# The function table of the RMS norms: one named set with logarithm and exponential, asked for ahead of the logarithm

## The chip, the cores and the metric

One Trainium2 chip, of which the kernel uses one core. The metric is the device time of one launch in microseconds, the median of several executions. Engines as the profile names them: PE is the matrix engine (TensorE) and PEld its weight loads, DVE is VectorE, ACT is ScalarE, POOL is GpSimd, SP is SyncE, which issues most DMAs. Each engine works through its own list of instructions in order and waits for the others by semaphores.

## The reference

One inference step of a two-layer decoder trunk for a prompt of 512 positions and a sample group of 8 x 4 positions, D_MODEL 1024, all in 32-bit floating point. What matters here are the norms: four per layer and group.

```python
def rms_norm(x, g):
    x32 = x.astype(jnp.float32)
    return x32 * lax.rsqrt(jnp.mean(x32 * x32, axis=-1, keepdims=True) + NORM_EPS) * g

def decoder_layer(x, start, st, prm):
    h = rms_norm(x, prm['g_mix_pre'])
    p_rw, p_s5, p_gdn, p_swa = split_cols(h @ prm['w_in'], PROJ_SPLITS)
    ...                                   # four mixers: RWKV-7, S5, gated DeltaNet, window attention
    mix = jnp.concatenate([o_rw, o_s5, o_gdn, o_swa], axis=-1) @ prm['w_out']
    x = x + rms_norm(mix, prm['g_mix_post'])
    h = rms_norm(x, prm['g_mlp_pre'])
    f = jnp.square(jax.nn.relu(h @ prm['w_up'])) @ prm['w_down']
    x = x + rms_norm(f, prm['g_mlp_post'])
    return x, ...
```

## The kernel before

Activations lie transposed: 128 partitions by 8 blocks of features by columns of positions. The 544 columns are cut into two halves, of 256 prompt columns and of 256 prompt plus 32 sample columns (288). Each dense product (`dense`, L1697) streams its weights from HBM in parts of 128 x 512: SP issues the load of `wraw` (L1656), ACT casts it to `whi` (L231), DVE forms the rest `wlo` (L235), and PE takes three groups of four matmuls for each part, whi and wlo with the two parts of the activation (L219; tiles `h` and `f` by name). The buffers are few (5 wraw, 3 whi, 3 wlo), so ACT, DVE and PE run in step. The four mixers add many small matmuls, elementwise work and DMAs. While one half is in a mixer, the other half's dense products fill PE.

A scheduler that has its own timeline sets the order on every engine: instructions are listed with priorities (`PRIO`, `ahead`, `section`), and the scheduler places each on its engine when its model has it ready. `after` (L185) adds an order between two instructions for the scheduler alone, with no semaphore at run time. A change of one instruction's place can so move others.

A norm is done in four steps. The squares of the features are summed into `sums` by ACT (Square, tile `d`) and POOL (L235). PE multiplies `sums` with a column of 1/1024 (`mean`), which leaves the mean in PSUM on all partitions. `rsqrt` (L1565) makes of it the factor `sums` = exp(-0.5 ln(mean + eps)) with two ACT instructions, `sums<-ps,eps` and `sums<-sums`. DVE then scales the row (L244, `d` or `c`), and what follows (a residual sum, or the cast to `h` or `f` by ACT, L231) goes on from there. There are 16 such norms; they are called norm 1 to norm 16 here, in the order in which ACT comes to them. Norm 1 is the first half's first norm, which has its own code in `first` (L1581), norm 2 the second half's; norms 3 to 15 are those between the products, and norm 16 is the last one, ahead of the output.

ACT evaluates a function from a set of tables that has to be loaded, by an ACT_TABLE_LOAD. Where the kernel doesn't ask for a set, the build puts a load in front of an activation whose function the set loaded last doesn't hold, after the order is fixed. Logarithm and exponential are so taken from two sets. Besides the norms the mixers use Exp, Tanh, Ln and Sin; copies, casts, squares and Relu need no load of their own.

Of the kernel before, what the change touches and what calls it, by code (L numbers as in the profile page):

```python
# [11 lines left out]
AF = mybir.ActivationFunctionType  # L12
# [126 lines left out]
class K:  # L139
# [1418 lines left out]
    def rms(self, sums):  # L1558

        n = sums.shape[1]  # L1560
        mp = self.ps([128, n], "mn")
        self.mm(mp, self.mean.to_broadcast([128, 128]), sums)
        return self.rsqrt(sums, mp)

    def rsqrt(self, out, mean):  # L1565
        self.act(out, mean, AF.Ln, bias=self.eps)
        self.last_exp = self.act(out, out, AF.Exp, scale=-0.5)
        return out

# [11 lines left out]
    def first(self, half):  # L1581

        c0, n = HALVES[half]
        x = self.big(half, "acc")
        for k in range(0, 8, 2):
            self.nc.sync.dma_start(out=x[:, k:k + 2], in_=self.x[half][:, k:k + 2])
        if not half:
            self.pfs = []
            for l in range(DEPTH):
                last = self.load_params(l)  # L1590
                self.pfs.append(self.pf)

            self.waiting = [last, self.load_consts()]
            self.pf = self.pfs[0]
        sums = self.row(half, "sums")
        if half:
            for k in range(8):
                self.square_sum(sums, k, x[:, k])
            return self.prenorm(half, x, "g_mix_pre", self.rms(sums))
        ps = self.ps([128, n], "mn")  # L1600
        for k in range(0, 8, 2):
            a, b = self.row(half), self.row(half, "c1")
            self.act(a, x[:, k], AF.Square)
            self.tt(b, x[:, k + 1], x[:, k + 1])
            self.tt(a, a, b, ALU.add)
            self.mm(ps, self.mean.to_broadcast([128, 128]), a, k == 0, k == 6)
        return self.prenorm(half, x, "g_mix_pre", self.rsqrt(sums, ps))

    def prenorm(self, half, x, g, sums, cls="h9"):

# [174 lines left out]
    def body(self):  # L1785
        self.pool("sb")
        self.pool("psum", space=PSUM)
        self.pool("dram", space=DRAM)
        self.x = [self.i["xT"][:, :, c0:c0 + n] for c0, n in HALVES]
        self.last_layer = False  # L1790
        self.carry = [{} for _ in range(DEPTH)]
        self.mix = {}
        self.last_gd = None
        self.mean = self.t([128, 1], "mean")
        self.nc.gpsimd.memset(self.mean, 1.0 / D)
        self.eps = self.t([128, 1], "eps")
        self.nc.gpsimd.memset(self.eps, NORM_EPS)
        self.nc.scalar.preload_act_table(AF.Ln)
        h = self.first(0)
        self.tables(0)  # L1800

        a, b = (self.w([128, 2304], "f9") for _ in range(2))
        xs = self.w([128, 2048], "acc")
        self.alt = dict(xs=xs, cv=a[:, 0:1536], sv=a[:, 1536:1792], gz=b[:, 0:512], us=b[:, 512:1024], sx=b[:, 1024:1792],
                        ba=b[:, 1792:2048])
        r = self.project(0, 0, h)
        zero = self.w([128, 520], "r4")
        self.nc.gpsimd.memset(zero, 0.0)
        self.diag = []
        for w in range(2):  # L1810
            self.diag.append([self.t([64 * 1040], f"diag{w}{x}", pool="dram") for x in range(2)])
            for d in self.diag[w]:
                self.nc.gpsimd.dma_start(out=d.rearrange("(p f) -> p f", p=128), in_=zero)
        self.alt = None
        h = self.first(1)
        self.mixers(r)
        for l in range(DEPTH):
            self.pf = self.pfs[l]
            self.last_layer = l == DEPTH - 1
            if not l:  # L1820
                r = self.project(l, 1, h)
                x = self.out_proj(l, 0)
            else:
                x = self.out_proj(l, 0)
                self.flush()
                r = self.project(l, 1, h["h"])
            self.mixers(r)
            xb = []
            other = lambda: xb.append(self.out_proj(l, 1))
            h = self.mlp(l, 0, x, other if l == DEPTH - 1 else None)  # L1830
            if not xb:
                other()
                self.flush()
            x = xb[0]
            if l + 1 < DEPTH:
                self.tables(l + 1)
                self.pf = self.pfs[l + 1]
                r = self.project(l + 1, 0, h["h"])
                self.mixers(r)
                self.pf = self.pfs[l]  # L1840
            h = self.mlp(l, 1, x)
        self.flush()
# [189 lines left out]
```

## Time and profile before

| | |
|---|---|
| median of 3 runs | 1700.71 us (1697.2 to 1704.5) |
| profiled execution | 1697.34 us, its span 1695.6 us |
| PE, PEld busy | 1575.9 us (93%), 1465.1 us (86%) |
| DVE, ACT, POOL busy | 1242.4 us (73%), 968.7 us (57%), 370.9 us (22%) |
| ACT_TABLE_LOAD | 72 in the page's group and one at the start of the program |
| granted TensorE clock, mean | 0.971 of full speed |

The span runs from the first to the last instruction; 1.7 us of the execution lie outside. PE is busy for most of it, so what counts is where PE stands still and what it waits for there. The profile says for each instruction how long its engine was idle ahead of it, and which instruction of which engine ended that wait. The granted clock is given for a stretch: 1.00 is 2.4 GHz, 0.50 is 1.2 GHz.

### The profile page before, as it was taken

Reading aid. Unit: us, or ns where it says so; the run is one execution under the profiler, and the core shown is the slowest. Engines: PE = TensorE matmul, PEld = TensorE weight load, DVE = VectorE, ACT = ScalarE, POOL = GpSimd, SP = SyncE. Lnnn points to the kernel's source line nnn. Section 1 sums busy time; section 2 is a strip of 40 time slices with the busy share of each in tenths; the row PEclk is TensorE's granted clock in tenths of the full one; section 3 lists DMA queues with packets and bytes.
Section 4 is the critical chain, followed back from the end, with each engine's and each line's share of the span. In section 5 each row is a group of like instructions: output and inputs, shape, how many; then the busy total and the mean of one; then the engine's idle time right before and its main releaser. Section 6 shows DMA issues by size and latency. Waiting matters only on the chain. (4 is left out here: it accounts for less than half of the span.)

```text
span 1695.6 us, 38309 instructions
## 1 busy us (share of the span) xinstructions
PE 1575.9 (93%) x14098; PEld 1465.1 (86%) x14098; DVE 1242.4 (73%) x3067; ACT 968.7 (57%) x2109; POOL 370.9 (22%) x689
## 2 busy tenths in 40 slices
PE   6998998689999899889999998989999999799996
PEld 5877987579888898879999997979899899799996
DVE  7888675976786858888576566879778755766665
ACT  5676557654436467766454457876444556655543
POOL 6461241200122615530001004620002101400002
PEclk9999999889999999999999999999999999999998
DMA  6644453443457547625346554534545766564452
GB/s 213 207 130 125 144 159 118 113 127 129 142 189 237 166 162 240 206 100 163 111 149 208 166 184 161 171 104 136 145 138 161 243 202 192 169 191 164 161 171 93
DMA packets 210184, 275.21 MB, mean 162 GB/s; under 512 B 78266, under 2 KB 101116, under 8 KB 209580
## 3 DMA queue, kind: packets, MB, share of 16 engines
q1 hardware_dynamic: 208076, 266.59, 49.7%
q0 software_dynamic: 1920, 6.17, 1.0%
q8 instruction: 110, 1.80, 0.4%
q14 instruction: 78, 0.64, 0.1%
HBM read 243.20 MB, written 31.21 MB: 162 GB/s over the span
## 5 line engine op out<-in xcount | busy, mean ns | idle before, releaser
L231 ACT CAST whi<-wraw 128x512 fp32r<-128x512 f32 x752 | 463.1, 619 | 431.6 <-PE ps L219 276.3
L235 DVE TENSOR_TENSOR wlo<-wraw,whi 128x512 fp32r<-128x512 f32 x752 | 540.5, 723 | 209.0 <-ACT whi L231 175.9
L219 PE MATMUL ps<-h,whi 128*128 128x288 f32 (+1 forms) x3264 | 519.0, 298 | 25.5 <-ACT h L231 22.1
L219 PEld LDWEIGHTS ps<-h,whi 128*128 128x128 f32 x3264 | 451.6, 192 | 43.4 <-ACT h L231 26.2
L219 PE MATMUL ps<-f,whi 128*128 128x288 f32 (+1 forms) x2752 | 429.9, 296 | 11.7 <-ACT f L231 5.6
L219 PEld LDWEIGHTS ps<-f,whi 128*128 128x128 f32 x2752 | 377.6, 192 | 24.6 <-ACT whi L231 8.3
L219 PE MATMUL ps<-h,wlo 128*128 128x288 f32 (+1 forms) x1632 | 289.5, 296 | 9.6 <-DVE wlo L235 8.8
L219 PEld LDWEIGHTS ps<-h,wlo 128*128 128x128 f32 x1632 | 236.1, 191 | 21.1 <-DVE wlo L235 13.6
L219 PE MATMUL ps<-f,wlo 128*128 128x288 f32 (+1 forms) x1376 | 237.4, 293 | 8.5 <-DVE wlo L235 8.0
L235 POOL TENSOR_TENSOR sums<-sums,d 128x288 f32<-128x288 f32 (+1 forms) x105 | 102.3, 976 | 561.8 <-ACT d L227 554.3
L219 PEld LDWEIGHTS ps<-f,wlo 128*128 128x128 f32 x1376 | 197.2, 191 | 14.8 <-DVE wlo L235 12.1
L227 ACT ACT_TABLE_LOAD x72 | 92.4, 1283 | 1.3
L219 PE MATMUL ps<-r,r 128*128 128x72 f32 (+7 forms) x800 | 86.6, 275 | 6.6 <-DVE r L235 2.4
L219 PEld LDWEIGHTS ps<-r,r 128*128 128x128 f32 (+4 forms) x800 | 69.1, 169 | 13.1 <-DVE r L235 2.5
L231 ACT CAST f<-d 128x256 fp32r<-128x256 f32 (+1 forms) x136 | 56.5, 416 | 37.8 <-DVE d L235 37.3
L235 DVE TENSOR_TENSOR acc<-acc,ps 128x256 f32<-128x256 f32 (+1 forms) x96 | 41.7, 434 | 46.1 <-PE ps L219 46.1
L227 ACT ACTIVATE d<-acc 128x288 f32<-128x288 f32 (+1 forms) x109 | 46.6, 431 | 40.1 <-DVE acc L235 26.8
L235 DVE TENSOR_TENSOR f<-d,f 128x256 fp32r<-128x256 f32 (+1 forms) x136 | 61.2, 451 | 5.3 <-ACT f L231 5.1
L235 DVE TENSOR_TENSOR d<-d 128x288 f32<-128x288 f32 (+1 forms) x128 | 60.1, 470 | 0.0
L244 DVE SCALAR_TENSOR_TENSOR d<-acc,pf,sums 128x256 f32<-128x256 f32 (+1 forms) x80 | 40.8, 524 | 19.7 <-ACT sums L227 18.2
L227 ACT ACTIVATE d<-ps 128x288 f32<-128x288 f32 (+1 forms) x128 | 50.4, 394 | 8.2 <-PE ps L219 7.8
L244 DVE SCALAR_TENSOR_TENSOR c<-acc,pf,sums 128x288 f32<-128x288 f32 (+1 forms) x48 | 27.3, 612 | 19.2 <-ACT sums L227 19.2
(380 smaller groups left out, 1832.0 us busy)
## 6 DMA issues: line engine op xcount, KB each, us to landing
wraw<-in_w_up SPq DMA_DIRECT2D x256, 256.0 KB, 2.7
wraw<-in_w_down SPq DMA_DIRECT2D x256, 256.0 KB, 2.9
wraw<-in_w_in SPq DMA_DIRECT2D x176, 256.0 KB, 3.1
wraw<-in_w_out SPq DMA_DIRECT2D x64, 256.0 KB, 2.9
r<-s5m SPq DMA_DIRECT2D x12, 512.0 KB, 5.3
t<-diag SPq DMA_DIRECT2D x32, 128.0 KB, 3.1
r<-s5kin SPq DMA_DIRECT2D x8, 512.0 KB, 5.6
x<-acc SPq DMA_DIRECT2D x3, 1152.0 KB, 5.4
```

Source lines behind the costliest of these rows:

```text
L219: return self.nc.tensor.matmul(out=out, lhsT=lhsT, rhs=rhs, start=start, stop=stop)
L227: return self.nc.scalar.activation(out=out, in_=in_, func=func, scale=scale, bias=bias, **kw)
L231: return self.nc.scalar.copy(out, in_)
L235: return (eng or self.nc.vector).tensor_tensor(out=out, in0=a, in1=b, op=op)
L244: return self.nc.vector.scalar_tensor_tensor(out=out, in0=a, scalar=s, in1=b, op0=op0, op1=op1)
```

## The change

`preload_act_table_set("natural_log_exp_and_others")` emits an ACT_TABLE_LOAD of a set that holds both functions. It is emitted once for each norm; by `after` the scheduler keeps it behind the mean's (last) matmul and ahead of the logarithm. Behind it, the build finds both functions in the loaded set and adds no load, as long as no function of another set stands between. The load at the start of the program takes the same set by name.

```diff
         mp = self.ps([128, n], "mn")
-        self.mm(mp, self.mean.to_broadcast([128, 128]), sums)
-        return self.rsqrt(sums, mp)
-
-    def rsqrt(self, out, mean):
-        self.act(out, mean, AF.Ln, bias=self.eps)
+        return self.rsqrt(sums, mp, self.mm(mp, self.mean.to_broadcast([128, 128]), sums))
+
+    def rsqrt(self, out, mean, dep):
+
+        t = self.nc.scalar.preload_act_table_set("natural_log_exp_and_others")
+        self.after(t, dep.ins)
+        self.after(self.act(out, mean, AF.Ln, bias=self.eps), t.ins)
         self.last_exp = self.act(out, out, AF.Exp, scale=-0.5)
...
-            self.mm(ps, self.mean.to_broadcast([128, 128]), a, k == 0, k == 6)
-        return self.prenorm(half, x, "g_mix_pre", self.rsqrt(sums, ps))
+            m = self.mm(ps, self.mean.to_broadcast([128, 128]), a, k == 0, k == 6)
+        return self.prenorm(half, x, "g_mix_pre", self.rsqrt(sums, ps, m))
...
-        self.nc.scalar.preload_act_table(AF.Ln)
+        self.nc.scalar.preload_act_table_set("natural_log_exp_and_others")
```

In the built programs ACT's list holds 73 table loads before and 60 after, 16 of these asked for by name in the norms (L1566). The rest of the instructions is the same in number. Their order is not: the scheduler has moved instructions on all engines in the stretches where a mixer and a dense product share PE; where a half runs dense products alone, PE's order is unchanged. Three places follow, in the program's own names.

DVE around norm 3, before. `sums_3742` is the norm's factor, the lines of L269 (ISA here, CUSTOM_DVE_ANT_0 in the trace) find the row maxima `swst` of the window attention's scores `g`, and `d<-acc` is the norm's first scaling:

```order
L269 ISA g_879_4510,swst_4509<-ps_4499,cst_77 128x256
L269 ISA swst_4509 128x1
L269 ISA g_879_4510,swst_4509<-ps_4499,cst_77 128x256
L269 ISA swst_4509 128x1
L244 SCALAR_TENSOR_TENSOR d_1135_5777<-acc_3741,pf_73,sums_3742 128x256
L244 SCALAR_TENSOR_TENSOR d_1137_5783<-acc_3741,pf_73,sums_3742 128x256
L538 COPY r_853_4364<-ps_4385 128x128
L235 TENSOR_TENSOR acc_3741<-d_1135_5777,xk_5775 128x256
L235 TENSOR_TENSOR c_849_4329<-t_848_4328,c_845_4324 64x2
L269 ISA g_880_4513,swst_4509<-ps_4500,cst_77 128x256
L269 ISA swst_4509 128x1
L269 ISA g_880_4513,swst_4509<-ps_4500,cst_77 128x256
```

And after:

```order
L269 ISA g_879_4512,swst_4511<-ps_4501,cst_77 128x256
L269 ISA swst_4511 128x1
L269 ISA g_879_4512,swst_4511<-ps_4501,cst_77 128x256
L269 ISA swst_4511 128x1
L538 COPY r_853_4366<-ps_4387 128x128
L269 ISA g_880_4515,swst_4511<-ps_4502,cst_77 128x256
L269 ISA swst_4511 128x1
L269 ISA g_880_4515,swst_4511<-ps_4502,cst_77 128x256
L269 ISA swst_4511 128x1
L244 SCALAR_TENSOR_TENSOR d_1135_5780<-acc_3743,pf_73,sums_3744 128x256
L244 SCALAR_TENSOR_TENSOR d_1137_5786<-acc_3743,pf_73,sums_3744 128x256
```

The second pair of maxima and a copy of `r` have moved from behind the norm's first two scalings to ahead of them.

ACT around norm 14, before. `sums_20032` is its factor, `d<-acc` are squares for the sum of norm 15 (which POOL adds up), `h<-c` is the cast that PE's next product needs:

```order
L231 CAST whi_20421<-wraw_20420 128x512
L227 ACTIVATE d_3989_20210<-acc_17378 128x256
L227 ACTIVATE d_3997_20251<-acc_17378 128x256
L227 ACT_TABLE_LOAD
L227 ACTIVATE sums_20032<-ps_20377,eps_65 128x288
L227 ACTIVATE d_4005_20292<-acc_17378 128x256
L227 ACT_TABLE_LOAD
L227 ACTIVATE sums_20032<-sums_20032 128x288
L231 CAST whi_20439<-wraw_20438 128x512
L227 ACTIVATE d_4013_20333<-acc_17378 128x256
L231 CAST whi_20506<-wraw_20505 128x512
L231 CAST h_4023_20381<-c_4025_20383 128x288
```

And after:

```order
L1566 ACT_TABLE_LOAD
L231 CAST whi_20435<-wraw_20434 128x512
L227 ACTIVATE d_3989_20223<-acc_17390 128x256
L227 ACTIVATE d_3997_20264<-acc_17390 128x256
L227 ACTIVATE sums_20045<-ps_20390,eps_65 128x288
L231 CAST whi_20453<-wraw_20452 128x512
L227 ACTIVATE sums_20045<-sums_20045 128x288
L227 ACTIVATE d_4005_20305<-acc_17390 128x256
L231 CAST whi_20521<-wraw_20520 128x512
L227 ACTIVATE d_4013_20346<-acc_17390 128x256
L231 CAST h_4023_20395<-c_4025_20397 128x288
```

The load ahead of the logarithm stands two squares earlier, the load behind it is gone, and a cast of weights stands between the two functions in its place.

PE at the first triangular inverse of the RWKV mixer, layer 0, first half, before. `t_362` is the inverse of the small blocks, which comes by DMA from `diag`, `t_352` the matrix; the `h,whi` and `h,wlo` rows are dense matmuls of the other half:

```order
L219 MATMUL ps_2807<-h_293_1471,whi_2809 128x288 x4
L219 MATMUL ps_2807<-h_294_1472,whi_2809 128x288 x4
L219 MATMUL ps_2807<-h_293_1471,wlo_2810 128x288 x4
L219 MATMUL ps_2807<-h_293_1471,whi_2827 128x288 x4
L219 MATMUL ps_2807<-h_294_1472,whi_2827 128x288 x4
L219 MATMUL ps_2807<-h_293_1471,wlo_2828 128x288 x4
L219 MATMUL ps_2153<-t_362_1732,t_352_1683 64x64
L219 MATMUL ps_2855<-h_293_1471,whi_2857 128x288 x4
L219 MATMUL ps_2855<-h_294_1472,whi_2857 128x288 x4
L219 MATMUL ps_2153<-t_362_1732,t_352_1683 64x64 x15
L219 MATMUL ps_1940<-g_397_1933,c_388_1896 64x256
```

And after:

```order
L219 MATMUL ps_2761<-h_294_1474,whi_2781 128x288
L219 MATMUL ps_2761<-h_293_1473,wlo_2782 128x288 x4
L219 MATMUL ps_1942<-g_397_1935,c_388_1898 64x256
L219 MATMUL ps_1942<-g_399_1940,c_388_1898 64x256
L219 MATMUL ps_1946<-f_85_438 128x128 x4
L219 MATMUL ps_2155<-t_362_1734,t_352_1685 64x64 x16
L219 MATMUL ps_2809<-h_293_1473,whi_2811 128x288 x4
L219 MATMUL ps_2809<-h_294_1474,whi_2811 128x288 x4
L219 MATMUL ps_1947<-f_85_438 128x128 x4
L219 MATMUL ps_2809<-h_293_1473,wlo_2812 128x288 x4
```

The 24 dense matmuls of one output tile (`ps_2807` before, `ps_2809` after) have moved from ahead of the inverse's first product `t,t` to behind it, and products of the window attention (`g,c` and `f`) from behind it to ahead.

## Rows read from the trace of the kernel before

**Rows 1.** The page: PE's busy time (share, count); then the group of table loads.

```profile
PE 1575.9 (93%) x14098; PEld 1465.1 (86%) x14098; DVE 1242.4 (73%) x3067; ACT 968.7 (57%) x2109; POOL 370.9 (22%) x689
...
L227 ACT ACT_TABLE_LOAD x72 | 92.4, 1283 | 1.3
```

**Rows 2.** Timeline, ACT and DVE, norm 16: start, us, what [idle before, what ended it].

```profile
1680.34 1.28 ACT L227 ACT_TABLE_LOAD   x1
...
1682.09 0.50 ACT L227 ACTIVATE sums<-ps,eps 128x288 f32<-128x288 f32 x1 [0.47 <-PE ps L219]
...
1682.61 1.28 ACT L227 ACT_TABLE_LOAD   x1
...
1684.45 2.34 DVE L244 SCALAR_TENSOR_TENSOR c<-acc,pf,sums 128x288 f32<-128x288 f32 x4 [4.67 <-ACT sums L227]
```

**Rows 3.** Timeline, ACT and PE, norm 1.

```profile
11.31 0.47 ACT L227 ACTIVATE sums<-ps,eps 128x256 f32<-128x256 f32 x1 [1.80 <-PE ps L219]
...
11.80 1.28 ACT L227 ACT_TABLE_LOAD   x1
...
13.10 0.42 ACT L227 ACTIVATE sums<-sums 128x256 f32<-128x256 f32 x1
...
14.52 1.23 PE L219 MATMUL ps<-h,whi 128*128 128x256 f32 x4 [3.31 <-ACT h L231]
```

**Rows 4.** Timeline, ACT and PE, around norm 2 (s5v: sines of layer 1's tables).

```profile
122.82 0.31 ACT L227 ACTIVATE s5v<-s5v 128x8 f32<-128x8 f32 x2 [0.42 <-DVE s5v L241]
...
132.17 1.18 PE L219 MATMUL ps<-h,whi 128*128 128x288 f32 x4 [2.65 <-ACT h L231]
```

**Rows 5.** Timeline, ACT, DVE and PE, norm 3.

```profile
319.79 1.28 ACT L227 ACT_TABLE_LOAD   x1
...
321.41 0.61 ACT L227 ACTIVATE r<-ps,cst 128x128 f32<-128x128 f32 x2
...
321.60 0.88 DVE L244 SCALAR_TENSOR_TENSOR d<-acc,pf,sums 128x256 f32<-128x256 f32 x2 [2.74 <-ACT sums L227]
...
323.00 0.41 DVE L269 CUSTOM_DVE_ANT_0 g<-ps,cst 128x256 f32<-128x256 f32 x1
...
330.62 1.09 PE L223 MATMUL ps<-cst,g 128*128 128x128 f32 x4 [6.74 <-DVE g L241]
```

**Rows 6.** Timeline, PE, norm 4.

```profile
342.35 1.22 PE L219 MATMUL ps<-h,whi 128*128 128x256 f32 x4 [3.32 <-ACT h L231]
```

**Rows 7.** Timeline, ACT and PE, norms 10 and 11.

```profile
1055.24 3.53 PE L219 MATMUL ps<-f,whi 128*128 128x288 f32 x10 [5.21 <-ACT f L231]
...
1055.61 0.43 ACT L231 CAST f<-c 128x288 fp32r<-128x288 f32 x1
...
1063.57 2.65 PE L219 MATMUL ps<-f,whi 128*128 128x288 f32 x14 [1.23 <-ACT whi L231]
```

**Rows 8.** Timeline, ACT and PE, norm 14.

```profile
1463.76 0.42 ACT L227 ACTIVATE d<-acc 128x256 f32<-128x256 f32 x1 [0.73 <-POOL sums L235]
...
1468.78 0.60 ACT L231 CAST whi<-wraw 128x512 fp32r<-128x512 f32 x1
...
1469.77 2.29 PE L219 MATMUL ps<-h,whi 128*128 128x288 f32 x8 [5.46 <-ACT h L231]
```

**Rows 9.** Timeline, PE, behind norm 7 and behind norm 9.

```profile
683.07 1.20 PE L219 MATMUL ps<-f,whi 128*128 128x256 f32 x8 [0.58 <-ACT whi L231]
...
1033.32 0.75 PE L219 MATMUL ps<-h,wlo 128*128 128x256 f32 x4 [0.63 <-DVE wlo L235]
```

**Rows 10.** Timeline, PE, the first triangular inverse.

```profile
147.79 1.09 PE L219 MATMUL ps<-h,whi 128*128 128x288 f32 x7
...
150.94 0.32 PE L219 MATMUL ps<-t,t 64*64 64x64 f32 x2
```

**Rows 11.** Stretches: length, each engine's busy us (count), granted clock, DMA share, GB/s.

```profile
140.00:310.00 170.00, 160.97 (x1661) 145.47 (x1660) 126.93 (x346) 103.24 (x245) 43.60 (x119) 0.99 0.44 136
310.00:346.00 36.00, 18.86 (x141) 14.06 (x140) 29.47 (x100) 21.25 (x53) 8.27 (x11) 0.69 0.51 131
```

## The prediction

> **What bounds the kernel now.** The page comes first: PE is busy for 1575.9 of 1695.6 us, and the table loads are 72 of 1283 ns, 92.4 us, on ACT, which is 57% busy [rows 1]. Off PE's path such a load costs nothing. So the second view is the list of PE's idle gaps in the timeline, and for each gap the chain behind it: is there a norm's logarithm and exponential in it, with the load between them? The third is the order of the built programs, which tells what stands in that chain now. The profiled execution took 1697.3 us, 3.4 under the median of the runs; the sum below is made against it and then taken off the median, 1700.7.
>
> **What one load costs.** Behind the logarithm of norm 1 the load begins 0.02 us after it ends (11.31 + 0.47 to 11.80) and the exponential begins 0.02 us after the load (11.80 + 1.28 to 13.10) [rows 3]. So 1.28 us are saved where ACT's next result is waited for, and nothing where it isn't. The Trainium skill, in "ScalarE: Activation LUTs", What ACT_TABLE_LOAD costs, puts some 1380 ns of drain on top of 1283 ns, 2.66 us for a switch. These rows leave no room for that drain; were it there in another form, each exposed load would give twice as much (rival 3).
>
> **The 13 loads fewer.** Norms 1 and 3 to 16 lose the load between their two functions. Some of that comes back: behind norms 7, 8 and 12 the mixers' Tanh needs a load that it didn't need before, since the set loaded last was then the exponential's. Some more goes where a mixer's own logarithm finds the set loaded. By the built order it is 13 in all. The load ahead of the logarithm stays, by name. The time follows from the places at which PE waits.
>
> - Norm 16, at the end: nothing else runs. The load ahead of the logarithm is hidden (ACT waits 0.47 us for the mean anyway); the one behind it lies between the logarithm and DVE, which waits 4.67 us [rows 2]. **1.28**, without a doubt.
> - Norm 1: PE waits 3.31 us for the cast `h`, with the load in the chain. The load by name, now a second one of the same set, falls into 1.80 us in which ACT waits for the mean [rows 3]. **1.28**.
> - Norm 4: PE waits 3.32 us for `h` by the same chain [rows 6]. **1.28**.
> - Norm 3 stands ahead of norm 4 with no dense work in between: from 310 to 346 us PE is busy for 18.86 of 36 us [rows 5, 11]. DVE waits 2.74 us for the exponential, and then works in one go through norm and softmax up to the 6.74 us wait of PE for the scaled `g`. The load (1.28) goes, two ACT instructions (0.61) now stand ahead of the exponential: 0.67 earlier. And DVE does the second pair of maxima (0.41 each) in its idle time instead of behind it: some 0.9 more. **1.6**, between 0.67 and 1.6.
> - Norm 10: PE waits 5.21 us for the cast `f`. A weight cast (0.60) [rows 8] stands where the load stood: 0.68. One square (0.42) has also moved from ahead of the logarithm to behind it: **1.1**, between 0.68 and 1.1.
> - Norm 11: PE waits 1.23 us for a weight cast behind the exponential [rows 7]. Two casts `f` (0.43 each) now stand there instead of the load: 1.28 - 0.86 = 0.42, **0.5**, between 0 and 1.23.
> - Norm 14: PE waits 5.46 us for `h`. Here too a weight cast takes the load's place, 0.68. The load ahead of the logarithm now stands ahead of two squares, the second of which waited 0.73 us for POOL [rows 8]: the load covers that wait. **1.4**, between 0.68 and 2.0.
> - Norms 7 and 9: PE waits 0.58 and 0.63 us for weight casts and their rests, delayed by the load [rows 9]. PE's wait bounds it; I take half, **0.6**, between 0 and 1.2.
> - The other norms (5, 6, 8, 12, 13, 15) stand beside dense work that runs on; I count them at nothing. Were that cover gone, each would give up to 1.28.
> - Norm 2 loses. Its load by name is followed at once in ACT's order by the load for the sines of layer 1's tables, which throws the set out; logarithm and exponential then each get a load as before. So there is one load more. ACT waited 0.42 us just there; the rest, 0.86, goes on through a busy ACT to PE's wait of 2.65 us for `h` [rows 4]. **-0.9**, between -1.28 and 0.
>
> Sum: 1.28 + 1.28 + 1.28 + 1.6 + 1.1 + 0.5 + 1.4 + 0.6 - 0.9 = **8.1 us**. With all low ends it is 4.5, with all high ends 11.2. What is late next in these chains is DVE's scaling (0.88 for two blocks [rows 5]) and ACT's cast (0.43 [rows 7]), which keep their length, and POOL's sums of squares. The granted clock was 0.69 in the stretch from 310 to 346 us [rows 11], where PE waits most, so much of it ran at 1.2 instead of 2.4 GHz; the eight matmuls after norm 14's wait took 2.29 us [rows 8] where eight others, somewhat narrower, took 1.20 [rows 9]. A shorter wait can give back about 1 us there, or nothing; I don't count it.
>
> **The order elsewhere.** The scheduler moved small matmuls against dense ones in all mixer stretches. From 140 to 310 us PE is idle for 9.0 us (170 - 160.97) [rows 11]; the total of products is the same, so a new order can only change idle time of that size, and the clock with it. I take zero for this with either sign open: it is the largest unknown here, and it sets the range. At the spot shown, the triangular inverse's first product began 3.15 us after the group of dense matmuls that stood ahead of it, and PE shows no wait for it [rows 10]; now that group is behind it. DVE's work on the inverse also stands three instructions earlier in its list, so the scheduler expects the data sooner.
>
> **Rivals.**
> 1. *The gain is given back.* The moved work opens waits of one or two us in three or four mixer stretches, or the removed loads only let ACT wait sooner for DVE and POOL. For it: POOL's sums and DVE bound several of these chains. Against it: norms 1, 4 and 16 can't lose their 3.8. Time: 1700.7 - 2 = 1698.7, between -4 and +4.
> 2. *Slower: the inverse's products come too early on PE.* PE works in order. If the DMA of `diag` is not there when PE reaches `t,t`, the dense group that used to cover it waits behind it, up to 3.15 us at this spot less the 0.9 by which PE itself is late there through norm 2, 2.2 us; the clock may fall then, and a mixer has two such inverses, each half and layer one mixer, eight in all. From a mean loss of 8.1 / 8 = 1.0 us each the kernel is slower than before, at 2.2 us by 17.6 - 8.1 = 9.5 us: 1710.2. Against it: not every inverse has moved this way, and the 8 stand in stretches whose order was made by the same scheduler in both programs.
> 3. *More than the sum.* All high ends and 1 us of clock at three places, 11.2 + 3 = 14.2: 1686.5. By the Trainium skill's figure for a switch (the page named above) an estimate would add 1.38 us at each of seven places with a load on the path (norms 1, 3, 4, 10, 11, 14, 16), 9.7 us, for some 1683; rows 3 speak against it, and it has 0.01 of this rival's chance.
> 4. *The set isn't used.* The build could put its own loads in spite of the one by name, as at norm 2; then 16 loads would come on top and the time would rise by up to 16 x 1.28 less what is hidden. The built order has no second load at the other 15 norms, so I give this no chance.
>
> **How the numbers follow.** Chances: forecast 0.56, rival 1 0.24, rival 2 0.12, rival 3 0.08. The forecast is 1700.7 - 8.1 = 1692.6, with 1689.5 to 1696.2 of its own. A measurement of this kernel can tell about 0.5%, 8.5 us, from no change, and the forecast stands just short of it. So of its 0.56 I count 0.26 as faster by more, 0.30 as within; rival 1 is within; of rival 2 0.10 is slower, 0.02 within; rival 3 is faster. Faster 0.34, same 0.56, slower 0.10. For the range, the lower end leaves out the far half of rival 3 and the forecast's own good order: 1684. The upper takes in rival 1 up to +2: 1703.
>
> **What would show it.** In the changed kernel's profile: 60 loads in all, 16 of them from the line that asks by name, so ACT has 13 x 1.28 = 16.7 us of loads less; at norm 16 the exponential starts right behind the logarithm and the tail from the mean to the end is 1.3 us shorter; PE's waits at norms 1 and 4 fall from 3.3 to about 2.0, at norm 14 from 5.5 to about 4, at norm 10 to about 4, the wait for `g` at norm 3 by 1.6 or more; at norm 2 PE resumes about 0.9 us later. PE's idle time falls by some 7 us outside the tail. It would be wrong if PE's idle time in the stretches from 140 to 310, 346 to 560, 700 to 860 and 1070 to 1290 us changes by more than 4 us in sum, or the granted clock by more than 0.005.

## The result, and the profile after

The changed kernel takes 1677.59 us (1669.5 to 1683.06, four runs) where the kernel before takes 1701.83 (1697.2 to 1704.5, four runs): ratio 0.9859, 95% interval [0.9824, 0.9895], some 24 us less. The forecast was 1692.6 with a range from 1684 to 1703. The direction was right, the size three times too small, and the time lies 6 us below the range.

The profiled execution took 1675.07 us with a span of 1673.3, against 1697.34 and 1695.6: 22.3 us less. Of the changed kernel, PE's row and the build's group of table loads from the page, and the named group from the list of ACT's lines, answer to [rows 1]:

```profile
PE 1576.6 (94%) x14098; PEld 1472.2 (88%) x14098; DVE 1245.0 (74%) x3067; ACT 952.2 (57%) x2096; POOL 373.9 (22%) x689
...
L227 ACT ACT_TABLE_LOAD x43 | 55.2, 1283 | 0.8
...
L1566 ACT ACT_TABLE_LOAD x16 | 20.5, 1283 | 0.3
```

With the one at the start that makes 60 loads, and ACT's busy time fell by 16.5 us. PE's busy time in sum is the same within 0.7 us (by stretch it moved both ways, as the first failed step below shows). So in sum the gain lies in what PE waits: up to its last matmul (at 1682.05 us before, 1661.04 after) PE stood idle for 106.2 us before and for 84.5 after. Four sums from the list of PE's waits (us in total, times, longest), first of the kernel before, then of the changed one:

```profile
PE ps L219 <- ACT h L231: 22.1, 10, 5.5
PE ps L219 <- DVE wlo L235: 16.9, 20, 3.7
...
PE ps L219 <- ACT f L231: 5.6, 2, 5.2
PE ps L219 <- DVE c L241: 5.5, 5, 1.8
```

```profile
PE ps L219 <- ACT h L231: 17.8, 10, 3.6
PE ps L219 <- DVE wlo L235: 9.8, 12, 1.5
...
PE ps L219 <- ACT f L231: 3.8, 2, 3.6
...
PE ps L219 <- DVE c L241: 2.3, 2, 1.3
```

The casts `h` and `f`, the ends of the norms' chains, give back 4.3 and 1.8 us, somewhat more than the 3.1 and 1.1 that the sum had for them. The largest fall, 7.1 us, is in waits for DVE's `wlo`, of which the sum says almost nothing (3.2 of it at 576 to 584 us, most of the rest beside norms); and `c` fell from 5.5 to 2.3 us.

All kernels here have the same 14,098 matmuls. Summed over equal numbers of them, PE's idle time shows where the time went (the stretches are given by the times of the kernel before; in the last line it is the time from the last matmul to the end):

| stretch, us | norms | idle before | after | gain | my sum |
|---|---|---|---|---|---|
| 0 to 122 | 1 | 18.5 | 16.9 | 1.6 | 1.28 |
| 122 to 156 | 2 | 6.4 | 6.8 | -0.4 | -0.9 |
| 314 to 350 | 3, 4 | 17.1 | 15.4 | 1.7 | 2.9 |
| 633 to 759 | 5 to 8 | 12.7 | 8.9 | 3.9 | 0.3 |
| 1027 to 1101 | 9 to 12 | 9.6 | 5.3 | 4.3 | 1.9 |
| 1441 to 1494 | 13 to 15 | 9.5 | 5.4 | 4.1 | 1.4 |
| all other | none | 32.4 | 25.8 | 6.5 | 0 |
| end | 16 | 13.5 | 12.3 | 1.3 | 1.28 |

That is 23.0 us, of which PE's busy time takes 0.7 back. In the stretches with norms the idle time fell by 16.5 us instead of 8.1, and away from them by 6.5 instead of nothing. Such a figure has its own scatter: in the kernel of experiment 5, whose list is that of the kernel before up to 900 us, the stretch from 633 to 759 had 10.7 us of idle time instead of 12.7; the difference lies in the mixer behind norm 8, from 705 us on.

The rows of the changed kernel that answer to the terms: norm 16 [rows 2] and norm 1 [rows 3] (timeline: start, us, what, [idle before, what ended it]):

```profile
1661.08 0.50 ACT L227 ACTIVATE sums<-ps,eps 128x288 f32<-128x288 f32 x1 [0.88 <-PE ps L219]
1661.61 0.44 ACT L227 ACTIVATE sums<-sums 128x288 f32<-128x288 f32 x1
1662.15 2.35 DVE L244 SCALAR_TENSOR_TENSOR c<-acc,pf,sums 128x288 f32<-128x288 f32 x4 [3.80 <-ACT sums L227]
```

```profile
9.23 1.28 ACT L1566 ACT_TABLE_LOAD   x1
...
11.39 0.47 ACT L227 ACTIVATE sums<-ps,eps 128x256 f32<-128x256 f32 x1 [0.87 <-PE ps L219]
...
11.89 0.42 ACT L227 ACTIVATE sums<-sums 128x256 f32<-128x256 f32 x1
...
13.32 1.23 PE L219 MATMUL ps<-h,whi 128*128 128x256 f32 x4 [2.03 <-ACT h L231]
```

The exponential follows the logarithm with no load between them, and PE's wait at norm 1 fell from 3.31 to 2.03, by 1.28 to the hundredth. The waits of PE at norms 2, 3 and 4, 10 and 14 [rows 4 to 8]:

```profile
131.14 1.44 PE L219 MATMUL ps<-h,whi 128*128 128x288 f32 x4 [2.47 <-ACT h L231]
...
330.13 1.09 PE L223 MATMUL ps<-cst,g 128*128 128x128 f32 x4 [6.58 <-DVE g L241]
...
339.17 1.22 PE L219 MATMUL ps<-sums,mean 128*128 128x256 f32 x2 [4.36 <-POOL sums L235]
...
342.36 1.23 PE L219 MATMUL ps<-h,whi 128*128 128x256 f32 x4 [1.97 <-ACT h L231]
...
1045.13 1.01 PE L219 MATMUL ps<-f,whi 128*128 128x288 f32 x4 [3.60 <-ACT f L231]
...
1449.48 2.23 PE L219 MATMUL ps<-h,whi 128*128 128x288 f32 x6 [3.59 <-ACT h L231]
```

The granted clock did not pay for it as a whole: its mean over the profiled execution was 0.971 before and 0.966 after. In the two stretches of [rows 11]:

```profile
140.00:310.00 170.00, 160.45 (x1638) 145.57 (x1636) 124.06 (x337) 102.52 (x241) 43.30 (x117) 0.97 0.44 135
310.00:346.00 36.00, 20.59 (x152) 15.63 (x152) 31.17 (x106) 19.47 (x54) 10.08 (x12) 0.71 0.51 131
```

### The profile page after: what moved, and what is told of

Read it like the earlier page. It is cut to its first block, busy times and chain, and to the rows that moved or that the text cites. A ratio compares the mean times of both kernels' runs of the same rounds, so it can differ in the third digit from the quotient of the medians.

```text
span 1673.3 us, 38301 instructions
## 1 busy us (share of the span) xinstructions
PE 1576.6 (94%) x14098; PEld 1472.2 (88%) x14098; DVE 1245.0 (74%) x3067; ACT 952.2 (57%) x2096; POOL 373.9 (22%) x689
## 5 line engine op out<-in xcount | busy, mean ns | idle before, releaser
L219 PE MATMUL ps<-f,whi 128*128 128x288 f32 (+1 forms) x2752 | 425.6, 294 | 9.6 <-ACT whi L231 4.7
L219 PEld LDWEIGHTS ps<-h,wlo 128*128 128x128 f32 x1632 | 238.7, 193 | 16.1 <-DVE wlo L235 11.2
L219 PE MATMUL ps<-r,r 128*128 128x72 f32 (+7 forms) x800 | 90.0, 281 | 4.5 <-DVE r L235 2.6
L231 ACT COPY r<-ps 64x128 f32<-64x128 f32 (+2 forms) x60 | 22.7, 383 | 27.3 <-PE ps L624 11.4
```

The source lines that it names most:

```text
L219: return self.nc.tensor.matmul(out=out, lhsT=lhsT, rhs=rhs, start=start, stop=stop)
L231: return self.nc.scalar.copy(out, in_)
```

## The experiments

Theory A: the time comes from loads that were on the path, at more places or dearer than I had it. Theory B: my 8 us for the loads were right, and the rest comes from the new order. Most experiments change only ACT's list of table loads, after the order of all engines is fixed; `edit` works on the finished program's list of instructions. Of each edit the lines that matter are shown.

**1. The order without the loads.** The changed kernel, its named loads taken out:

```diff
...
+    loads = [i for i in L if type(i).__name__ == "InstLoadActFuncSet"]
+    for i in loads[1:]:
+        L.remove(i)
```

> The order of the changed kernel on every engine, but the sixteen named loads are taken out once the order is fixed, so logarithm and exponential are again loaded apart: 70 loads instead of 60 (73 in the kernel before). Theory A, the loads: the 22.3 us of span come from loads that no longer lie on the path, at more places or at a higher price than my sum had. Then this kernel takes about what the kernel before takes, ratio 0.998 to 1.002. Theory B, the order: my 8 us for the loads were about right, and the other 14 us come from the new order alone. Then this kernel is still some 14 us faster than the kernel before, ratio 0.990 to 0.993.

Measured: 1693.83 us against 1703.14, ratio 0.9940 [0.9917, 0.9963]; PE's idle time 102.4 us. The new order alone is faster, by some 10 us (6 to 14 by the interval), though it still has 70 loads. Only 3.8 us of that show as idle time, and the two profiled spans differ by 2.4 us, because the profiled execution of the kernel before was one of its faster ones. Away from the norms PE's idle time fell by 1.1 us here, where the change has 6.5.

**2. The loads without the order.** The kernel before, with the named load directly ahead of each of the 16 logarithms (`norms` lists them):

```diff
...
+    for ln in norms(L):
+        nc.scalar.preload_act_table_set("natural_log_exp_and_others")
+        L.insert(L.index(ln), end.pop())
```

> The order of the kernel before on every engine, with one load of the named set put directly ahead of each of the sixteen logarithms once the order is fixed: 62 loads instead of 73. Theory A (loads alone): some 20 us faster than the kernel before, ratio 0.987 to 0.989, and PE's waits fall at places that my sum left out. Theory B (order): the terms of my sum without their shares of moved work, 1.28 each for norms 1, 3, 4, 10, 14, 16, 0.5 to 1.2 for norm 11, 0.6 for norms 7 and 9, and a gain instead of the loss at norm 2, up to 1.28: some 9 to 11 us, ratio 0.993 to 0.995. A rival C: each half of the effect needs the other, and the two single effects don't add up to 24 us.

Measured: 1691.01 us against 1703.14, ratio 0.9911 [0.9884, 0.9939], between the two theories; PE's idle time 94.1 us, 12.1 less, and 1.3 less from the last matmul to the end. (Its profiled execution, 1682.54 us, is the fastest of its runs; so the time is taken from the ratio, and the places from the idle time.) The product of the two ratios is 0.985, the change's is 0.986. In time the two halves just add up. In PE's idle time they do more than that: 12.1 + 3.8 = 15.9 against 21.7. The named loads gave 3.1 us around norms 9 to 12 in the old order (9.6 to 6.5) and 5.2 in the new one (10.5 to 5.3). The times can't tell whether this part, rival C, is real. One difference besides the order is seen in the lists: here the load stands directly ahead of the logarithm, in the changed kernel one to six other ACT instructions stand between the two at norms 5 to 14. Norm 6, first in this kernel, then in the changed one:

```profile
643.09 1.28 ACT L2027 ACT_TABLE_LOAD   x1
644.38 0.47 ACT L227 ACTIVATE sums<-ps,eps 128x256 f32<-128x256 f32 x1
```

```profile
645.45 1.28 ACT L1566 ACT_TABLE_LOAD   x1
646.74 1.14 ACT L231 CAST whi<-wraw 128x512 fp32r<-128x512 f32 x2
647.79 0.47 ACT L227 ACTIVATE sums<-ps,eps 128x256 f32<-128x256 f32 x1
```

No run has the early load in the old order; experiment 11 below bears on what its place is worth.

**3. Norm 2.** The changed kernel, with norm 2's load moved directly ahead of its logarithm:

```diff
...
+    L.remove(loads[2])
+    L.insert(L.index(lns[1]), loads[2])
```

> The changed kernel with one load moved in ACT's list: norm 2's named load stands directly ahead of its logarithm instead of ahead of the sines that throw its set out, so two loads fall away in norm 2 (one comes back later, at a mixer's Tanh: 59 instead of 60 in all). By my step for norm 2 (0.9 us lost there to the useless load) PE comes out of its wait for h there 0.9 us earlier, and up to 1.28 more since logarithm and exponential no longer have a load between them: 1 to 2.2 us faster than the changed kernel. If the time isn't made there (ACT or PE has slack behind the norm), no difference.

Measured: 1671.30 us, ratio to the kernel before 0.9810 [0.9785, 0.9835], against 0.9859 [0.9824, 0.9895] of the change. The list of this kernel has 59 loads. PE's wait for `h` at norm 2 is now:

```profile
130.76 1.33 PE L219 MATMUL ps<-h,whi 128*128 128x288 f32 x4 [1.02 <-ACT h L231]
```

That is 1.02 instead of 2.47 us, and PE's idle time there fell by 1.4 us, in all by 1.65. That lies within what was expected of the step. The other 4 to 5 us between the two medians lie in runs that differ by 13 us for one and the same kernel, so they are not put down to it.

**4. One load more at every norm.** The kernel before, with a load of another set between logarithm and exponential:

```diff
...
+        nc.scalar.preload_act_table_set("natural_log")
+        L.insert(L.index(exp), end.pop())
```

> The order of the kernel before, with a second load between logarithm and exponential at each of the sixteen norms (another set, so that the exponential's own load stays): 90 loads instead of 73. It prices one more load in each of these chains. By my sum, 1.28 us each at norms 1, 2, 3, 4, 10, 14 and 16, some 1 at 11, 0.6 at 7 and 9 together, nothing elsewhere: 10 to 11 us slower than the kernel before, ratio 1.006 to 1.0065. If a load on the path costs more than its 1.28 us (what is behind it waits longer, PE's clock falls), or at more norms than I counted, 16 to 25 us slower, ratio 1.010 to 1.015: that would speak for theory A.

Measured: 1724.77 us, ratio 1.0124 [1.0099, 1.0150], 21.6 us for 17 loads. In the profile PE's idle time rose by 12.4 us, its busy time by 11.1 at a mean granted clock of 0.962 instead of 0.971, and the tail by 1.3. So more norms are exposed than my sum said. The price of a load itself is not larger: two in a row stand 1.29 us apart, as the rows of experiment 10 show below.

**5. Sixteen loads beside plain dense work.** The kernel before, with loads ahead of weight casts far from any norm:

```diff
...
+    for i in spots[3::8][:16]:
+        nc.scalar.preload_act_table_set("exp_and_others")
+        L.insert(L.index(i), end.pop())
```

> The order of the kernel before, and sixteen loads more that change no later load (89 instead of 73): seven of them ahead of weight casts in the second layer-1 dense stretch (some 900 to 1000 us) and nine in the last one (1480 to 1680 us), far from any norm. Seventeen loads more at the norms cost 21.5 us. If a load is hidden beside plain dense work, as my prediction took it to be beside all dense work, these cost nothing: ratio 0.998 to 1.002. Then what failed is that the dense work next to a norm is not such cover. If ACT has no slack anywhere, they cost 16 x 1.28 = 20 us, ratio 1.012.

Measured: 1700.67 us against 1699.64, ratio 1.0003 [0.9984, 1.0022]. Two of its stretches (length, then busy us and count of PE, PEld, DVE, ACT and POOL, the granted clock, DMA share, GB/s):

```profile
900.00:1000.00 100.00, 99.76 (x752) 99.12 (x751) 61.55 (x119) 58.69 (x103) 1.98 (x6) 1.00 0.56 184
1490.00:1670.00 180.00, 179.99 (x1356) 179.76 (x1355) 110.22 (x200) 105.88 (x195) 1.83 (x3) 1.00 0.54 171
```

PE runs on with 0.25 us of idle time in 280. Here a load costs nothing that shows.

**6 and 7. Two neighbouring orders.** The kernel before with one priority nudged, in each of two kernels:

```diff
-PRIO = {..., 'load': 294, ...}
+PRIO = {..., 'load': 295, ...}
...
-PRIO = {..., 'gd1': 200, ...}
+PRIO = {..., 'gd1': 201, ...}
```

> The kernel before with one scheduler priority nudged (that of the loads, 294 to 295): same instructions, 73 table loads as before, another order in some mixer stretches. It asks whether an order by itself moves the time by several us. If the scheduler's choice among near-equal orders is a lottery of the size seen (the changed kernel's order alone gave 9 us, 6.5 us of it in PE's idle time), the time moves by 3 to 10 us in either direction. If orders of this scheduler are all about equal and the changed kernel's order is better for a reason that lies in the change (it plans with the load at its place), the time stays within 3 us.

> The same question with another nudge of the kernel before (priority of a mixer's first stage, 200 to 201): 73 table loads, another order. Lottery: 3 to 10 us in either direction, not the same as the other nudge. No lottery: within 3 us.

Measured: 1714.52 us, ratio 1.0073 [1.0046, 1.0100], and 1718.37 us, ratio 1.0106 [1.0074, 1.0137]. Same instructions, same 73 loads, by the ratios 12 and 18 us slower. In their profiled executions the mean granted clocks were 0.967 and 0.956 (the second is the slowest of its six runs), PE's idle time 110.5 and 111.5 us. Four orders of nearly the same program so lie 28 us apart by their ratios. (The 6.5 us that the first expectation gives to the order's idle time are the change's; the order alone had 3.8 in all.)

**8 and 11. The fewest loads.** All loads chosen anew along the list, each for the longest run of functions to come, once in the changed kernel's order (27 loads) and once in that of the kernel before (29 loads):

```diff
...
+        run = {s: next((n for n, j in enumerate(acts[k:]) if j.func not in f), len(acts)) for s, f in SETS.items()}
+        best = max(run, key=run.get)
+        nc.scalar.preload_act_table_set(best)
+        L.insert(L.index(i), end.pop())
```

> The changed kernel's order, with all table loads chosen anew once the order is fixed: at each function that the resident set lacks, the one of three sets (exponential and tanh; logarithm and exponential; sine) is loaded that serves the longest run of functions to come. 27 loads instead of 60. At the norms there is one load, as in the changed kernel, or none. If only the norms' loads lie on the path and the mixers' loads are covered, the time is that of the third experiment (1671 us, norm 2 mended), ratio 0.981. If the mixers' loads are exposed like the norms' (17 loads more there cost 21.5 us, about their full price), 33 loads fewer than the changed kernel give up to 33 x 1.28 = 42 us; by halves, since the mixers run beside dense work, 20 us: some 1655 us, ratio 0.972.

> The order of the kernel before, with the loads chosen by the longest run, as in the eighth experiment: 29 loads instead of 73. In the changed kernel's order 32 loads fewer outside the norms made no difference that could be told. If that holds in this order too, the time is that of the second experiment (ratio 0.991). If it was a matter of that order, up to some 10 us less, ratio 0.985.

Measured: 1671.02 us, ratio 0.9820 [0.9791, 0.9848], and 1674.45 us, ratio 0.9834 [0.9809, 0.9859]. Together with the first two experiments:

| ratio to the kernel before (PE idle, us) | loads by the build | one named load per norm | longest run |
|---|---|---|---|
| order before | 1 (106.2) | 0.9911 (94.1) | 0.9834 (86.1) |
| order of the change | 0.9940 (102.4) | 0.9859 (84.5) | 0.9820 (78.0) |

With the fewest loads the two orders can't be told apart by time. In the new order, 32 loads fewer than with norm 2 mended bring nothing that can be measured; in the old order 33 fewer bring some 13 us more than the named loads alone. Both kernels, and the one with norm 2 mended, are faster than the change by their medians; their intervals overlap among each other and with the change's, so none of them is shown to be the best.

**9 and 10. Eight norms beside dense work, six of them counted at nothing.** The kernel before, once with the named load at norms 5, 6, 7, 8, 9, 12, 13 and 15 only, once with one load more at these:

```diff
...
+        own = n in (5, 6, 7, 8, 9, 12, 13, 15)
+        nc.scalar.preload_act_table_set("natural_log_exp_and_others" if own else "natural_log")
+        L.insert(L.index(ln), end.pop())
...
+        if n in (5, 6, 7, 8, 9, 12, 13, 15):
+            nc.scalar.preload_act_table_set("natural_log")
+            L.insert(L.index(exp), end.pop())
```

> The order of the kernel before; the single named load only at norms 5, 6, 7, 8, 9, 12, 13 and 15, the eight that stand beside dense work, at six of which my prediction counted nothing (0.6 us for norms 7 and 9). The other eight keep their two loads. If the step was right, half a microsecond, ratio 0.999 to 1.000. If ACT is what these stretches wait for (it was busy for 17.0 of the 20 us from 645 to 665 us in the kernel before), 3 to 5 us, ratio 0.997 to 0.998: PE's waits there were 0.2 to 1.2 us long, so a load of 1.28 us can't give its whole length back.

> The order of the kernel before, with a second load between logarithm and exponential at the same eight norms only (82 loads instead of 73). A load that comes on top can't find a wait that is shorter than itself, so it shows the cover more plainly than one taken away. If dense work covers ACT there, 0, ratio 0.999 to 1.001. If not, up to 8 x 1.28 = 10 us, ratio 1.005 to 1.006.

Measured: 1698.85 us against 1701.14, ratio 0.9979 [0.9962, 0.9997], and 1710.69 us, ratio 1.0049 [1.0029, 1.0069]. The second is clear: 9.5 us for nine loads (norm 8 takes two), so dense work does not cover ACT there. In its trace the same matmul comes 1.3 us later behind each of norms 5, 9, 12, 13 and 15 than ahead of it, and 2.4 and 2.8 behind norms 6 and 7. (PE's idle time rose by 6.5 us around these seven norms, and by 2.4 in all, since it fell in mixer stretches that have the same list.) The first is small, and its time of itself tells little from my half microsecond; PE's idle time fell by 4.4 us in all and by 2.3 around the seven norms. Norm 6 of the kernel with one load more:

```profile
657.44 1.28 ACT L2030 ACT_TABLE_LOAD   x1
658.73 1.28 ACT L227 ACT_TABLE_LOAD   x1
660.03 0.42 ACT L227 ACTIVATE sums<-sums 128x256 f32<-128x256 f32 x1
...
661.52 1.65 PE L219 MATMUL ps<-f,whi 128*128 128x256 f32 x4 [1.63 <-ACT f L231]
```

and in the kernel before:

```profile
655.58 1.42 PE L219 MATMUL ps<-f,whi 128*128 128x256 f32 x4 [0.34 <-ACT f L231]
```

1.63 - 0.34 = 1.29: the load comes through to PE whole.

## Why the prediction was wrong

**What held.** The bound (PE's gaps, and the norm's chain behind them), the price of a load where it is exposed, the 13 loads, and the terms with nothing beside them: norm 16, norm 1 and norm 4 (3.32 to 1.97) gave 1.28 to 1.35 each. Norm 2 lost 0.4 us of idle time against this profile, and 1.0 to 1.6 against four other kernels with the old list there (experiments 1, 5, 9 and 10), where 0.9 was said; that its cause was the right one fits experiment 3. Norm 14 gave 1.87 of a stated 1.4, norm 10 1.61 of 1.1, of which 0.37 came back in two short waits right behind it. The 17 loads of experiment 4 cost 21.6 us, 1.27 each, and the two loads above leave no room for a drain. The Trainium skill, "ScalarE: Activation LUTs", What ACT_TABLE_LOAD costs, gives 2.66 us for a switch, which would make an estimate of 45 us for these 17; the runs do not bear it out. The sum's outer ends add up to 4.6 and 11.0 us, not to 4.5 and 11.2; that changes nothing here.

**The step that failed first: "The other norms (5, 6, 8, 12, 13, 15) stand beside dense work that runs on; I count them at nothing."** Around norms 5 to 15 the sum had 3.6 us. Every kernel has the same matmuls from 633 to 705, 1027 to 1101 and 1441 to 1494 us of the kernel before (all norms from 5 to 15 but norm 8). The time from the start of the first of them to the start of the first one behind, summed over the three stretches:

| kernel | us less than the kernel before |
|---|---|
| the change | 16.5 |
| 1, the new order alone | 0.8 |
| 2, loads directly ahead of the logarithm, old order | 9.9 |
| 11 and 8, fewest loads, old and new order | 15.8, 16.1 |
| 10, one load more at seven of these ten norms | -11.6 |
| 4, one load more at all ten | -13.1 |
| 5, loads elsewhere | 0.05 |

So here it is the loads, and not the order. Norms 5, 6, 12, 13 and 15, counted at nothing, gave some 8 us of the 16.5; norms 7 and 9, which "PE's wait bounds" at 1.2, gave some 4. Norm 8's stretch, 705 to 759 us, became 1.9 us shorter, but 2.1 with the order alone. That experiment 2 falls short of the change by 6 us while experiment 11, in the same old order, does not, speaks for the place of the load that is left: of these norms the prediction gave its move something at norm 14 alone. It was not tested by itself. A stop of PE also costs more than its idle time. From 633 to 705 us the clock was full in both kernels, and besides 2.4 us of idle time the same matmuls lost 3.0 us of busy time (before, after; the first busy time is that of PE):

```profile
633.04:705.11 72.07, 68.52 (x524) 63.92 (x523) 61.31 (x109) 55.35 (x123) 31.21 (x52) 1.00 0.65 215
```

```profile
631.61:698.35 66.74, 65.56 (x524) 63.21 (x522) 59.86 (x107) 52.98 (x121) 31.82 (x53) 1.00 0.72 234
```

I had looked at PE, which runs on there, and not at ACT. These are stretches of the kernel before around norms 6 and 12, and one of plain dense work between them, with the fourth busy time that of ACT:

```profile
645.00:665.00 20.00, 18.62 (x130) 16.27 (x130) 14.79 (x30) 17.04 (x38) 5.71 (x7) 1.00 0.76 253
900.00:1000.00 100.00, 99.37 (x749) 98.92 (x749) 63.13 (x125) 52.18 (x105) 0.00 (x0) 1.00 0.52 171
1082.00:1096.00 14.00, 13.83 (x100) 13.43 (x101) 11.35 (x29) 12.96 (x35) 9.88 (x21) 1.00 0.71 235
```

Around norm 6 ACT is busy for 85% of the stretch, around norm 12 for 93%, in plain dense work for 52%. The busy share alone does not decide it: around norm 5 (632 to 645 us) it is 68%, and there too one load more came through whole. What ACT itself waits for tells more. In the plain stretch from 900 to 1000 us its weight casts wait 24.9 us for PE to set a buffer free, so ACT is ahead of PE; from 645 to 665 us, around norm 6, they wait 0.2:

```profile
ACT whi L231 <- PE ps L219: 24.9, 26, 4.5
...
ACT whi L231 <- PE ps L219: 0.2, 1, 0.2
```

Copies out of PSUM, squares and casts of the norm stand in the same list as the weight casts, so ACT has little lead over PE left, and a load becomes PE's wait. This is a sign and not a measure: around norms 9 and 13 the casts wait for PE for 1.7 and 1.8 of 14 us, and one load more still came through whole. Where ACT has its lead, sixteen loads cost nothing (experiment 5). Taking the load between the two functions away gives only a part back (4.8 us in these stretches in experiment 9); it is one load more that shows the full price (experiment 10).

**The step that failed second: the order elsewhere, taken as zero.** I named it the largest unknown, and then let it move the range by 4 us either way. The order alone gave some 10 us, and two nudges cost 12 and 18. Two places in the trace, both away from the norms, gave 7.5 us of idle time or more in every kernel with the new order; elsewhere some of it was lost again. In experiment 1 a wait of 3.70 us for a mixer's `c` around 1331 us took half of it; a wait of the same kind, 3.52 us, stands in experiment 4, in the old order. So no more than these two places is shown.

At 576 to 584 us of the kernel before PE waited three times for `wlo`, 1.5 us each; of the changed kernel, once (1.40). DVE's and POOL's rows there, before:

```profile
575.57 3.02 POOL L235 TENSOR_TENSOR r<-s 64x512 f32<-64x512 f32 x2
...
575.70 1.75 DVE L235 TENSOR_TENSOR wlo<-wraw,whi 128x512 fp32r<-128x512 f32 x1
577.37 1.50 DVE L235 TENSOR_TENSOR f<-d,f 128x256 fp32r<-128x256 f32 x1
...
577.50 0.75 PE L219 MATMUL ps<-h,wlo 128*128 128x256 f32 x4 [1.54 <-DVE wlo L235]
```

and after, when POOL's row of products has ended earlier in the dense work:

```profile
576.67 3.02 POOL L235 TENSOR_TENSOR r<-s 64x512 f32<-64x512 f32 x2
...
580.16 0.41 DVE L235 TENSOR_TENSOR f<-d,f 128x256 fp32r<-128x256 f32 x1
580.50 0.68 DVE L235 TENSOR_TENSOR wlo<-wraw,whi 128x512 fp32r<-128x512 f32 x1
```

While POOL's tensor products run, DVE needs 1.75 us for a `wlo` that takes 0.68 alone, and 1.50 for an `f` that takes 0.41. The new order puts POOL's row of products some parts of the weights earlier, before the dense product comes to the blocks where DVE has `d` and `f` to do as well. The idle time of this stretch (560 to 590 us) is 5.0 to 5.2 us in all kernels with the old order (any loads, and both nudges) and 2.0 in all with the new one.

At 1123 to 1128 us PE waited in the kernel before for `c` of a mixer:

```profile
1124.18 0.68 PE L219 MATMUL ps<-cst,c 128*128 128x130 f32 x4 [1.08 <-DVE c L241]
...
1127.71 1.04 PE L219 MATMUL ps<-cst,c 32*128 32x40 f32 x4 [1.84 <-DVE c L241]
...
1120.00:1135.00 15.00, 11.87 (x56) 9.03 (x55) 9.51 (x30) 12.16 (x31) 0.80 (x1) 0.77 0.24 72
```

The last row is the stretch from 1120 to 1135: a mean granted clock of 0.77, so nearly half of it at 1.2 GHz, around the two waits. With the new order these products stand behind more dense work, there is no wait, and the same stretch reads:

```profile
1105.00:1120.00 15.00, 15.00 (x99) 13.06 (x98) 13.48 (x37) 13.45 (x35) 3.07 (x2) 1.00 0.42 124
```

Over the 500 matmuls there, idle time fell from 5.3 to 0.9 us and busy time from 67.1 to 63.2, with the new order and the old loads too (0.8 and 63.2). With the old order and the fewest loads both waits are still there, 1.08 and 1.84. So this is the order, not the loads.

**Norm 3: the mechanism, but not the place.** I expected 1.6 us off the wait for `g`. That wait stayed (6.74 to 6.58); a wait of 2.10 ahead of it, for other products, went. Then 1.84 were given back: PE's wait for POOL's `sums`, the mean of norm 4, grew from 2.52 to 4.36. Of the kernel before:

```profile
322.74 1.15 PE L219 MATMUL ps<-r,r 64*64 64x64 f32 x32 [2.10 <-DVE r L538]
...
337.81 1.22 PE L219 MATMUL ps<-sums,mean 128*128 128x256 f32 x2 [2.52 <-POOL sums L235]
```

In the old order with the named loads, norms 3 and 4 gave 2.7 us, in the new one 1.7. This is rival 1, at one place.

**The rivals.** Rival 2 did not come: the longest wait of PE for an inverse's `t` in the changed kernel is 0.69 us. Rival 3, more than the sum, was the right one in direction, with 0.08, but it put the surplus into the clock and into dearer loads, where it was not: the mean clock was no higher, and a load costs 1.28. I had said that PE's idle time outside the tail would fall by some 7 us; it fell by 21.7. The sum of the changes in the mixers' stretches was to refute me from 4 us on; over the same matmuls it was 7.5 us in the change and 4.3 with the order alone.

**What stays open.** Whether the new order is better for a reason that lies in the change (the scheduler sees a named load and its length, but not one that the build adds later), or by luck: the two other orders were both slower, which fits either. Whether the early place of the load alone makes up what experiment 2 lacks. Why the order alone gave some 9 us between the medians, with 3.8 us less idle time. And why the two orders take about the same time with the fewest loads, though PE's idle time still differs by 8 us; the mean granted clock was 0.970 in the old order and 0.965 in the new one.

## What to carry to other kernels

Whether a step on an engine is covered is asked of that engine: look in the very stretch whether it waits, and long, for the engine it feeds (then it has a lead), and price the step by adding one more of it there, since a removed one gives back no more than the stops that are left, and these cost more than the idle time shown. A change that lets a scheduler plan anew is two changes; hold the order fixed to measure the first, and give the second a range from a neighbouring order or two. Where two functions share a set, one load by name pays on the path, and one that another function's load throws out again costs.

## What the runs showed of the hardware that was not expected

DVE and POOL slowed each other as if they took turns. From 572 to 585 us of the kernel before, each DVE operation with two inputs in SBUF that began beside one of POOL's ended 0.3 to 0.6 us after POOL's had ended, at two and a half to four times its length alone. The Trainium skill, "SBUF — State Buffer", SBUF: two separate sides, calls the port pair that the two engines share an exclusive lock, held for the whole instruction, for which a DVE operation with two inputs in SBUF contends with a POOL operation that reads it. The trace agrees (1.75 against 0.68 us).

The executions of one program differ with the clock granted: the changed kernel took 1669.5 us at a mean of 0.971, 1675.1 at 0.966, 1680.1 at 0.965 and 1683.1 at 0.963. That is more than half of what the change gave, so effects of 3 us were read here from PE's idle time and from the same matmuls' starts, not from the times. In one and the same list the idle time of a mixer's stretch moved too, by 2 us from 705 to 759 us.
